# Order of the work at three places of a two-layer decoder trunk: the end of stick-breaking attention, the weight sums of the feed-forward blocks, and the rotary tables

## The chip, the cores and the metric

The kernel runs on one core of one Trainium2 chip. The metric is the device time of one execution in microseconds (us), taken as the median of several runs; lower is better. The core has five engines that this text names by the profile's abbreviations: PE (TensorE, the matrix multiplier), DVE (VectorE), ACT (ScalarE), POOL (GpSimd) and SP (SyncE, which here issues the DMA transfers). Each engine takes its own instructions in the order in which they were put in its list, and waits for others through semaphores.

## The reference

The program is a trunk of two layers on a sequence of 512 tokens of width 1024, all in float32. Each layer is a chain of four sub-layers, each between two RMS norms and added to the residual stream `h`:

- a gated feed-forward block, `silu(x @ w_gate) * (x @ w_up) @ w_down`, with 2816 hidden features, added at half weight
- a token mixer: in the first layer multi-scale retention with rotary queries and keys (4 heads), in the second layer stick-breaking attention (8 heads of 128)
- a second feed-forward block like the first
- a gate on a per-layer input embedding

Stick-breaking attention computes, for a query i and the keys j before it, the scores `z`, the running sums of `log_sigmoid(-z)` from j up to i, and the weights `exp(log_sigmoid(z) + rem)`; the weights times the values give each head's context, and all heads' contexts together are multiplied by one output matrix:

```
log_one_minus = where(mask, log_sigmoid(-z), 0)
rem = cumsum(log_one_minus, reverse) - log_one_minus
a = where(mask, exp(log_sigmoid(z) + rem), 0)
out = concat_heads(a @ v) @ w_out
```

The rotary tables are the sine and the cosine of position times frequency; only retention uses them.

## The kernel before

*Precision.* Each float32 operand is split into a high and a low part (`split`: ACT copies the high part, line 153, and DVE subtracts it from the operand, line 154), and a product is three matmuls, high by high, high by low and low by high (`mm3`, lines 159 to 161). So each weight that comes from memory costs one ACT and one DVE operation on a tile of 128 x 1024 before PE can use it.

*Weights.* `plan` writes down the list of all weight pieces in the order in which PE uses them, and PE's programme takes them from it one by one (`take`). `_fetch` has SP load a piece into one of 8 raw buffers, `_load` splits it into one of 5 buffer pairs (`wh`, `wl`; `HL_BUFS`), and `_ahead` keeps as many pieces loaded as buffers are free: piece n takes the buffers of piece n-5. Some pieces have a home elsewhere in the on-chip memory.

*Feed-forward blocks.* 22 hidden blocks of 128 features are made in pairs 0 to 10. Pair 0 is computed plainly. For pairs 1 to 10 the gate and the up projection use a scheme with seven products instead of eight (`gate_up`, 24 matmuls at line 728 for each product): it needs sums of the input quarters (made once in each block, on DVE, in `pre`) and sums of the pair's four raw weight tiles `b[0, 0]`, `b[1, 0]`, `b[0, 1]`, `b[1, 1]`. The products of a pair come in the order 1, 2, 6, 5, 7, 3, 4. The weight sums are made in `_load` when product 6's piece is loaded: `t1`, and two more in place, three DVE operations on 128 x 1024 (line 247), and a fourth after product 6's split. A product's result is taken from its PSUM bank by an ACT copy or by a DVE add into `y` (line 687), and a bank that holds products 1, 6, 7 and 4 in turn is read after each, so that product 4 can't start before the add of product 7. The down projections of an earlier group of pairs are put between the products of the later pairs (`ffn_steps`).

*Rotary tables.* `rope_tables` makes them with 24 DVE and 3 ACT operations on 128 x 512, from the positions that SP loads, and has SP store them in two DRAM tiles. The call stands at step 50 of the 86 steps of the first layer's first feed-forward block, near the products of pair 6, but nothing that it reads is made there.

*Attention's end.* `last_products` runs when the last head, 7, is left. `sums(7)` makes its running sums, `context(6)` and `context(7)` are the last contexts (`oT`, split by ACT and DVE), and `product(half, t, heads)` multiplies the contexts of the given heads for one row tile t of 128 tokens by their part of the output matrix: three matmuls of 512 columns for each head. Half 0 of the output's columns takes heads 4 to 7, half 1 heads 2 to 7; the heads before were added into `part` earlier. The products of a tile and half go to one PSUM bank. `close_a` ends half 0 of a tile: DVE adds the bank to `part` (line 558), ACT squares and sums (line 524), POOL multiplies by the gain (line 528). `close_b` does the same for half 1 (lines 565, 538, 539) and ends with POOL's power (line 541). `run_c` then does the residual on DVE (line 546) and the next norm's squares on ACT (line 460) and POOL (451, 452), `run_d` the scaling on DVE (line 464), and `flush` the transposes on PE (line 470) that make the input of the next block.

*What sets the order.* A scheduler orders each engine's list when the program is built: an operation is put in the list when its inputs are ready by the scheduler's own times, earlier traced work first. Three things override it: inside `traced` PE keeps the written order; `chained` ties each operation of the norm chains behind the one before it on its engine; and `issue_after(ins)` puts what is traced inside it behind `ins` in the list of the same engine. That is an order of issue and no wait for an end. It doesn't touch other engines.

The loop at the end of attention, as it is before:

```python
for t in range(NT):
    product(0, t, range(4, h))
context(h)
product(1, 0, range(2, h))
for t in range(NT):
    product(0, t, (h,))
    ssa[t] = self.close_a(t, pss[0][t], gpost, False)
self.done_with(2)
for t in range(NT):
    if t:
        product(1, t, range(2, SH - 3))
    self.run_c()
```

Of the kernel before, what the change touches and what calls it, by code (L numbers as in the profile page):

```python
# [21 lines left out]
NT = S // P  # L22
# [25 lines left out]
def ffn_steps():  # L48

    out = [("gu", 1, 1), ("gu", 1, 2), ("down", 0, 0, 0), ("down", 0, 1, 0), ("gu", 2, 1), ("gu", 2, 2)]  # L50
    out += [("gu", p, prod) for p in (1, 2) for prod in ORDER[2:]]
    out += [("gu", 3, prod) for prod in ORDER]
    for g in range(2, len(GROUPS)):
        gu = [("gu", p, prod) for p in range(*GROUPS[g]) for prod in ORDER]
        down = [("down", g - 1, half, q) for half in range(2) for q in range(*GROUPS[g - 1])]
        at = [int((i + 0.7) * len(gu) / len(down)) for i in range(len(down))]
        if g == len(GROUPS) - 1:

            at = [int((i + 0.7) * (len(gu) - 3) / len(down)) for i in range(len(down))]
        for i, x in enumerate(gu):  # L60
            out.append(x)
            out += [d for d, a in zip(down, at) if a == i]
    return out
# [17 lines left out]
class Trunk:  # L81
# [148 lines left out]
    def piece(self, x, w, home=None):  # L230
        if home and home[0] == "blk":
            parts = [self.blk2() for _ in range(2)]
            for i, hl in enumerate(parts):
                self.split(hl, x[:, i * 512 : i * 512 + 512])
            return tuple(Parts(p) for p in zip(*parts))
        if home and home[0] in ("xe", "xs"):
            h, l = (getattr(self, home[0])[:, 2 * home[1] + i] for i in range(2))
        elif home:
            h, l = (self.work.tile([P, 1280], F32R, tag="pk", name="pk", bufs=self.npacks)[:, :w] for _ in range(2))
        else:  # L240
            h = self.hl.tile([P, 1024], F32R, tag="wh", name="wh")[:, :w]
            l = self.hl.tile([P, 1024], F32R, tag="wl", name="wl")[:, :w]
        self.split((h, l), x)
        return h, l

    def sub(self, out, a, b, op=ALU.subtract):
# [2 lines left out]
    def _load(self):  # L249
        n = self.loaded  # L250
        item = self.items[n]
        self._open(n)
        if item[0] == "w":
            x = self.packs.pop(n)
            self.queue[n] = self.piece(x, 1024, self.home.get(n))
        elif item[0] == "st":
            _, key, prod = item
            b = self.packs[key]
            if prod == 6:
                w = b[0, 0].shape[-1]  # L260
                b["t1"] = self.sums.tile([P, 1024], F32, tag="t1", name="t1")[:, :w]

                with self.tc.issue_after(self.s_sums):
                    self.sub(b["t1"], b[0, 1], b[0, 0])
                    self.sub(b[0, 0], b[1, 1], b["t1"])
                    self.sub(b[0, 1], b[1, 1], b[0, 1])
            x = {1: b[0, 0], 2: b[1, 0], 3: b[1, 1], 4: b[0, 0], 5: b.get("t1"), 6: b[0, 0], 7: b[0, 1]}[prod]
            self.queue[n] = self.piece(x, x.shape[-1])
            if prod == 6:
                self.sub(b[0, 0], b[1, 0], b[0, 0])  # L270
        self.loaded += 1
# [413 lines left out]
    def ffn(self, layer, j, gpost, after, side=None):  # L685
# [102 lines left out]
        with self.traced():  # L788
            for n, x in enumerate(ffn_steps()):
                if n == 50 and side:  # L790
                    side()
                (gate_up if x[0] == "gu" else down)(*x[1:])
                if x[:2] == ("gu", NPAIR - 1) and x[2] in ORDER[2:]:
                    self.open_home(self.LAST[ORDER.index(x[2]) - 2])
# [191 lines left out]
    def stick(self, layer, gpost, after):  # L986
# [85 lines left out]
        def sums(h):  # L1072

            b, r = z.pop(h)
            for i, (at, w) in enumerate(BANK):
                group(b[i][:, :w], [(self.ntri, x[:, at : at + w]) for x in L[h]], False)
            for jj in range(1, NT):
                for j in range(jj):
                    group(r[j][:, (jj - j) * P :], [(self.nones, seg(x, jj)) for x in L[h]], False)
            e = pack()  # L1080
            for i, (at, w) in enumerate(BANK):
                nc.scalar.activation(e[:, at : at + w], b[i][:, :w], AF.Exp)
            mask(e)
            a[h] = pack(F32R), pack(F32R)
            self.split(a[h], e)

        def context(h):
            ps = self.ps()
            for j in range(NT):
                vj = [x[:, (j % 2) * 256 + (h % 2) * P : (j % 2) * 256 + (h % 2) * P + P] for x in v[h // 2, j // 2]]  # L1090
                self.mm3(ps[:, j * P :], vj, [seg(x, j) for x in a[h]], j == 0, j == NT - 1)
            oT[h] = self.blk2()
            self.split(oT[h], ps)
# [36 lines left out]
        h = SH - 1  # L1130

        def last_products():
            sums(h)
            pss = [[self.ps() for _ in range(NT)] for _ in range(2)]
            self.open_home(*(("pk", i) for i in range(3)))
            us0 = [self.unit("sb_w_out", idx, 512 + 256 * i, 2, 0, 512) for i in range(2)]
            specs = [("sb_w_out", idx, 256 + 256 * i, 2, 512, 512) for i in range(3)]
            self.begin_chain()
            us1 = [self.unit(*spec) for spec in specs]

            def product(half, t, heads):
                for hd in heads:
                    h0 = 4 - 2 * half
                    u = (us0, us1)[half][(hd - h0) // 2]
                    self.mm3(pss[half][t], stat(hd)(0, t), [x[:, hd % 2, :] for x in u], hd == h0, hd == h)

            for t in range(NT):
                product(0, t, range(4, h))
            context(h)
            product(1, 0, range(2, h))  # L1150
            for t in range(NT):
                product(0, t, (h,))
                ssa[t] = self.close_a(t, pss[0][t], gpost, False)
            self.done_with(2)
            for t in range(NT):
                if t:
                    product(1, t, range(2, SH - 3))
                self.run_c()
                if t == NT - 1:
                    self.flush()  # L1160
                product(1, t, range(SH - 3, SH) if t else (h,))
                if t == NT - 1:
                    self.done_with(3)
                self.close_b(t, pss[1][t], gpost, False, ssa[t], after)
                self.run_d()
                if t == 2:
                    self.flush(1)
            self.run_c()
            self.run_d()

        with self.traced():
            last_products()
# [177 lines left out]
```

## Time and profile before

| | |
|---|---|
| median of 3 runs | 2220.15 us (2218.29 to 2221.09) |
| the profiled execution: its time, its span | 2220.81 us, 2218.9 us |
| PE busy | 2174.7 us, 98% of the span |
| DVE busy | 1466.0 us, 66% |
| ACT busy | 1003.4 us, 45% |
| POOL busy | 236.7 us, 11% |
| mean granted PE clock | 0.995 of full speed |

The span is from the first to the last instruction of one execution. A row of a timeline has the start in us, the duration, the engine, the line, the operation, what it writes and reads by the program's names (`t`, `raw`: weights and their sums; `wh`, `wl`: the split; `xs`, `xe`: the input's quarters and their sums; `y`: results of products), its shape, how many were merged, and in brackets how long the engine stood idle before it and what ended that. Matmuls overlap, so their durations are longer than the distance from one start to the next. A row of the table by stretch gives busy time and number of instructions of PE, PE's weight loads, DVE, ACT and POOL in that stretch, and then the granted PE clock, the share of the DMA engines and their GB/s. A row of a group ends with busy time, mean duration and idle time before. A row of the chain has the start, the length and the work on it.

### The profile page before, as it was taken

Reading aid. Unit: us, or ns where it says so; the run is one execution under the profiler, and the core shown is the slowest. Engines: PE = TensorE matmul, PEld = TensorE weight load, DVE = VectorE, ACT = ScalarE, POOL = GpSimd, SP = SyncE. Lnnn points to the kernel's source line nnn. Section 1 sums busy time; section 2 is a strip of 40 time slices with the busy share of each in tenths; the row PEclk is TensorE's granted clock in tenths of the full one; section 3 lists DMA queues with packets and bytes.
Section 4 is the critical chain, followed back from the end, with each engine's and each line's share of the span. In section 5 each row is a group of like instructions: output and inputs, shape, how many; then the busy total and the mean of one; then the engine's idle time right before and its main releaser. Section 6 shows DMA issues by size and latency. Waiting matters only on the chain.

```text
span 2218.9 us, 32989 instructions
## 1 busy us (share of the span) xinstructions
PE 2174.7 (98%) x13640; PEld 1962.7 (88%) x13640; DVE 1466.0 (66%) x1739; ACT 1003.4 (45%) x1476; POOL 236.7 (11%) x337
## 2 busy tenths in 40 slices
PE   8999999999999999999999999999999989999998
PEld 7899998888888899999988999998988889999986
DVE  7976676553535588577766976776554568767764
ACT  5543444232223355344555544444555455444443
POOL 0000003110111210000032000002131220000031
PEclk9999999999999999999999999999999999999999
DMA  5323335231322324322453233235312232333341
GB/s 214 127 102 97 106 121 181 91 106 60 110 76 81 124 96 134 114 97 94 143 201 131 87 116 112 98 103 171 115 58 77 86 115 95 105 105 105 114 162 57
DMA packets 69415, 248.83 MB, mean 112 GB/s; under 512 B 7952, under 2 KB 7952, under 8 KB 69264
## 3 DMA queue, kind: packets, MB, share of 16 engines
q1 hardware_dynamic: 69264, 246.72, 33.6%
q8 instruction: 107, 1.75, 0.3%
q14 instruction: 44, 0.36, 0.1%
HBM read 229.38 MB, written 17.30 MB: 111 GB/s over the span
## 4 chain that ended last, share of the span: by engine, by line
PE 88%; DVE 6%; ACT 2%; issue 1%; POOL 1%; DMA 1%; SPq 0%; DVEq 0%; POOLq 0%; ACTq 0%
PE ps L728 33%; PE ps L160 18%; PE ps L159 18%; PE ps L161 18%; PE ps L1042 1%; DVE wl L154 1%; DMA raw<-wts 1%; DVE raw L247 1%; DVE xs L154 1%; PE ps L470 1%; DVE part L546 0%; DVE xe L154 0%; DVE y L687 0%; ACT xn L460 0%; POOL st L541 0%
## 5 line engine op out<-in xcount | busy, mean ns | idle before, releaser
L154 DVE TENSOR_TENSOR wl<-raw,wh 128x1024 fp32r<-128x1024 f32 x427 | 526.6, 1239 | 356.2 <-ACT wh L153 353.5
L153 ACT ACTIVATE wh<-raw 128x1024 fp32r<-128x1024 f32 x427 | 449.8, 1059 | 640.5 <-PE ps L728 202.2
L728 PE MATMUL ps<-xs,wh 128*128 128x256 f32 x2560 | 464.7, 283 | 6.7 <-DVE y L687 6.6
L728 PEld LDWEIGHTS ps<-xs,wh 128*128 128x128 f32 x2560 | 399.0, 189 | 11.0 <-DVE y L687 7.9
L728 PE MATMUL ps<-xs,wl 128*128 128x256 f32 x1280 | 362.9, 284 | 0.0
L728 PE MATMUL ps<-xe,wh 128*128 128x256 f32 x1920 | 350.5, 284 | 0.0
L728 PEld LDWEIGHTS ps<-xe,wh 128*128 128x128 f32 x1920 | 302.3, 193 | 1.9
L728 PE MATMUL ps<-xe,wl 128*128 128x256 f32 x960 | 272.8, 284 | 4.3 <-DVE wl L154 4.3
L159 PE MATMUL ps<-wh,blk 128*128 128x512 f32 x680 | 266.3, 392 | 1.9 <-ACT blk L153 1.9
L161 PE MATMUL ps<-wh,blk 128*128 128x512 f32 x680 | 265.2, 391 | 1.1 <-DVE blk L154 1.1
L160 PE MATMUL ps<-wl,blk 128*128 128x512 f32 x680 | 266.0, 391 | 0.0
L728 PEld LDWEIGHTS ps<-xs,wl 128*128 128x128 f32 x1280 | 242.3, 189 | 0.0
L728 PEld LDWEIGHTS ps<-xe,wl 128*128 128x128 f32 x960 | 184.9, 193 | 4.5 <-DVE wl L154 4.5
L160 PE MATMUL ps<-xs,wh 128*128 128x256 f32 (+1 forms) x576 | 186.1, 323 | 2.2 <-DVE xs L154 2.2
L159 PE MATMUL ps<-xs,wh 128*128 128x256 f32 (+1 forms) x576 | 186.5, 324 | 0.2 <-ACT xs L153 0.2
L161 PE MATMUL ps<-xs,wl 128*128 128x256 f32 (+1 forms) x576 | 185.3, 322 | 0.0
L161 PE MATMUL ps<-wh,xs 128*128 128x512 f32 (+1 forms) x448 | 162.9, 364 | 0.0
L159 PE MATMUL ps<-wh,xs 128*128 128x512 f32 (+1 forms) x448 | 162.7, 363 | 0.0
L160 PE MATMUL ps<-wl,xs 128*128 128x512 f32 (+1 forms) x448 | 162.6, 363 | 0.0
L526 POOL TENSOR_SCALAR st<-st 128x1 f32<-128x1 f32 x32 | 8.9, 279 | 1375.0 <-ACT junk L524 1358.9
L161 PEld LDWEIGHTS ps<-wh,blk 128*128 128x128 f32 x680 | 128.0, 188 | 28.7 <-DVE blk L154 1.5
L159 PEld LDWEIGHTS ps<-wh,blk 128*128 128x128 f32 x680 | 128.2, 189 | 26.8 <-ACT blk L153 2.1
(169 smaller groups left out, 3443.8 us busy)
## 6 DMA issues: line engine op xcount, KB each, us to landing
raw<-wts SPq DMA_DIRECT2D x382, 512.0 KB, 3.5
keep<-part SPq DMA_DIRECT2D x28, 512.0 KB, 4.2
rin<-keep SPq DMA_DIRECT2D x28, 512.0 KB, 4.1
gbc<-gains SPq DMA_DIRECT2D x16, 512.0 KB, 3.8
part<-x SPq DMA_DIRECT2D x4, 512.0 KB, 7.7
rin<-x SPq DMA_DIRECT2D x4, 512.0 KB, 4.9
out<-part SPq DMA_DIRECT2D x8, 256.0 KB, 2.2
dec<-decay SPq DMA_DIRECT2D x4, 256.0 KB, 3.7
```

The source lines that it names most:

```text
L153: h = self.nc.scalar.activation(hl[0], x, AF.Copy)
L154: l = self.nc.vector.tensor_tensor(out=hl[1], in0=x, in1=hl[0], op=ALU.subtract)
L159: mm(ps, a[0], b[0], start=start, stop=False)
L160: mm(ps, a[0], b[1], start=False, stop=False)
L161: mm(ps, a[1], b[0], start=False, stop=stop)
L247: self.nc.vector.tensor_tensor(out=out, in0=a, in1=b, op=op)
L470: nc.tensor.transpose(ps[:, c * P : (c + 1) * P], xn[:, (4 * q + c) * P : (4 * q + c + 1) * P], self.ident)
L526: nc.gpsimd.tensor_scalar(out=r, in0=ss, scalar1=1.0, scalar2=(4 if half else 1) * RMS_EPS, op0=ALU.mult, op1=ALU.add)
L728: nc.tensor.matmul(o, w[a][:, g, k, :], x[b][:, k, :], start=new and g + k + n == 0, stop=k == 3 and n == 2, skip_group_check=True)
L1042: nc.tensor.matmul(ps, l, m, start=fresh and i == 0, stop=i == len(pairs) - 1, skip_group_check=True)
```

## The change

Three edits, which add no operation and remove none:

1. The last DVE operation of a split is kept as `last_piece` when a piece goes to ordinary buffers, and a pair's three weight sums are issued behind it on DVE, beside the older tie to the sums of the input (`s_sums`).
2. The rotary tables' operations are issued behind the split that was traced last at their place: its ACT part for the ACT operations, its DVE part for the DVE ones. The DMA issues of SP are not tied.
3. At attention's end PE's order changes: the products of heads 4 and 5 of half 0 come first for all four row tiles, then head 6 of tiles 0 and 1, heads 2 to 5 of half 1 of tile 0, `context(7)`, the rest of head 6, and then the loop over row tiles does half 0's head 7 with `close_a` and half 1 with `close_b` tile by tile, where half 0 was closed for all tiles first.

```diff
@@ piece
         self.split((h, l), x)
+        self.last_piece = self.split_ins[1].ins
         return h, l
@@ _load
-                with self.tc.issue_after(self.s_sums):
+                with self.tc.issue_after(self.s_sums), self.tc.issue_after(self.last_piece):
                     self.sub(b["t1"], b[0, 1], b[0, 0])
                     self.sub(b[0, 0], b[1, 1], b["t1"])
                     self.sub(b[0, 1], b[1, 1], b[0, 1])
@@ ffn
                 if n == 50 and side:
-                    side()
+                    with ExitStack() as stack:
+                        for i in self.split_ins:
+                            stack.enter_context(self.tc.issue_after(i.ins))
+                        side()
@@ last_products
             for t in range(NT):
-                product(0, t, range(4, h))
+                product(0, t, (4, 5))
+            for t in range(2):
+                product(0, t, (6,))
+            product(1, 0, range(2, 6))
             context(h)
-            product(1, 0, range(2, h))
+            for t in range(2, NT):
+                product(0, t, (6,))
+            product(1, 0, (6,))
             for t in range(NT):
                 product(0, t, (h,))
+                if t == NT - 1:
+                    self.done_with(2)
                 ssa[t] = self.close_a(t, pss[0][t], gpost, False)
-            self.done_with(2)
-            for t in range(NT):
                 if t:
                     product(1, t, range(2, SH - 3))
                 self.run_c()
```

## The prediction

> **What bounds the kernel now.** I read the page first, then TensorE's (PE's) timeline for breaks in its stream, then what VectorE (DVE), ScalarE (ACT), GpSimd (POOL) and SyncE (SP) did at each break, and last a table by stretch.
>
> ```profile
> PE 2174.7 (98%) x13640; PEld 1962.7 (88%) x13640; DVE 1466.0 (66%) x1739; ACT 1003.4 (45%) x1476; POOL 236.7 (11%) x337
> ...
> core 0: us, PE busy (x) PEld busy (x) DVE busy (x) ACT busy (x) POOL busy (x), PEclk, DMA share, GB/s
> 64.40:100.90 36.50, 31.82 (x243) 31.21 (x242) 35.03 (x42) 19.44 (x28) 0.00 (x0) 0.91 0.44 145
> 854.90:861.40 6.50, 5.88 (x49) 5.67 (x48) 6.50 (x9) 2.84 (x4) 0.00 (x0) 1.00 0.01 3
> 1250.50:1274.20 23.70, 20.54 (x170) 20.13 (x169) 20.76 (x24) 11.26 (x16) 0.00 (x0) 1.00 0.35 108
> 1870.00:1881.50 11.50, 8.98 (x63) 8.78 (x62) 10.48 (x14) 4.12 (x7) 0.00 (x0) 0.85 0.03 7
> 1757.20:1799.40 42.20, 33.48 (x144) 27.11 (x144) 22.05 (x25) 15.83 (x31) 13.09 (x20) 0.92 0.38 123
> ...
> 858.56 28.83 PE ps L728 x240
> ...
> 1875.67 30.36 PE ps L728 x240
> ```
>
> PE is the bound: it works nearly all the time, so a change pays only where PE stands still. Two rows of the chain give the pace of the feed-forward products, 28.83/240 = 0.120 us a matmul, 2.9 us for the 24 of one product. With it the first four stretches give what PE lost: 36.5 - 243 x 0.120 = 7.3 us; 6.5 - 5.9 = 0.6; 23.7 - 20.4 = 3.3; 11.5 - 7.6 = 3.9. They are the same place in the four feed-forward blocks, where pairs 1 to 3 begin; together 15.1 us. The fifth stretch, attention's end, holds 114 products 512 wide (0.23 us each, rows below), 12 of `context(7)` (about 1.8 us by their widths) and 16 transposes (0.11 us each): 29.6 us of work in 42.2, so 12.6 us lost. All else has no break worth a term. These 27.7 us are the most that this change can win.
>
> **The change part by part.**
>
> *Pair sums behind the last piece.* What PE waits for in the third stretch:
>
> ```profile
> 1253.28 0.28 PE L728 MATMUL ps<-xe,wl 128*128 128x256 f32 x1
> 1255.27 0.39 PE L728 MATMUL ps<-xs,wh 128*128 128x256 f32 x1 [1.71 <-DVE y L687]
> ...
> 1252.26 1.23 DVE L247 TENSOR_TENSOR t<-raw 128x1024 f32<-128x1024 f32 x1 [2.55 <-DMA raw<-wts]
> 1253.40 1.22 DVE L154 TENSOR_TENSOR wl<-t,wh 128x1024 fp32r<-128x1024 f32 x1
> 1254.53 0.68 DVE L687 TENSOR_TENSOR y<-y,ps 128x512 f32<-128x512 f32 x1
> ...
> 1264.82 1.23 DVE L247 TENSOR_TENSOR t<-raw 128x1024 f32<-128x1024 f32 x1 [1.19 <-DMA raw<-wts]
> ...
> 1869.18 1.23 DVE L247 TENSOR_TENSOR t<-raw 128x1024 f32<-128x1024 f32 x1 [2.27 <-DMA raw<-wts]
> ```
>
> DVE runs in order. At 1249.7 it stood before `t1` of pair 3, whose weights had not landed; behind it waited a split of pair 2 and the add `y` that empties the bank in which PE must go on (product 4 of pair 1 after product 7). `t1` of pair 3 is needed eight products later, 8 x 2.9 = 23 us. Twice more the same: 1264.82 (pair 4) and 1869.18. With the tie, pair 3's three sums follow the split of (3, 2). That split takes the buffer that PE frees when it ends (2, 5), so it can't be early: without the break PE starts (1, 4) at 1253.4 and ends (2, 5) three products on, at 1262.1, and the split follows at about 1263.5; pair 3's weights have landed by 1252.3. So the DMA waits leave DVE's path, and the break with them. The new price: three sums of 1.14 us pitch and the split of product 6 now come in a row. From (2, 5)'s end: ACT's `wh` 1.06, split 1.14, `t1` to +3.6; `y` of (2, 7) is ready at about +3.1 and due at +5.7, so it goes in after `t1`, before the two sums that need `t1` finished. The sixth product's split ends at about +8, due at +14. No break follows by these numbers; if `y` went behind all three sums it would be 0.9 late. I take 0.2 in each block. From pair 4 on, down-projections of 5.5 us lie between, or the buffer comes free one product later, after `y`. Taken: 0.6 + 3.3 + 3.9 - 0.6 = 7.2 us (bounds 3.3, the three DMA waits of the rows less 0.9 in each block, to 7.8).
>
> *Rotary tables.*
>
> ```profile
> 64.41 0.40 PE L728 MATMUL ps<-xe,wh 128*128 128x256 f32 x2
> 69.09 0.58 PE L728 MATMUL ps<-xe,wl 128*128 128x256 f32 x1 [4.28 <-DVE wl L154]
> 69.47 0.63 PE L728 MATMUL ps<-xe,wh 128*128 128x256 f32 x2
> ...
> 57.65 2.37 DVE L247 TENSOR_TENSOR t<-raw 128x1024 f32<-128x1024 f32 x2
> 63.99 1.24 DVE L247 TENSOR_TENSOR raw<-raw,t 128x1024 f32<-128x1024 f32 x1
> 67.80 1.24 DVE L154 TENSOR_TENSOR wl<-raw,wh 128x1024 fp32r<-128x1024 f32 x1
> ...
> L410 DVE SCALAR_TENSOR_TENSOR rope<-rope x10: 686/694/706, 30.1 to 74.9; 128x512 f32<-128x512 f32 x10
> L406 DVE TENSOR_SCALAR rope<-rope x4: 417/425/437, 28.7 to 66.3; 128x512 f32<-128x512 f32 x4
> ...
> 29.00:69.00 40.00, 35.28 (x251) 32.99 (x250) 39.93 (x60) 25.77 (x38) 0.00 (x0) 0.98 0.09 30
> 220.00:240.00 20.00, 20.00 (x138) 18.65 (x138) 13.73 (x17) 8.12 (x12) 0.00 (x0) 1.00 0.42 132
> 240.00:260.00 20.00, 20.00 (x147) 19.04 (x146) 16.85 (x20) 8.70 (x12) 0.00 (x0) 1.00 0.17 56
> ```
>
> DVE has almost no idle time from 29 to 69 us, and PE waits 4.28 us at 69.09 for the split of (1, 6) at 67.80. Ahead of that split, in the saturated time, stand some 17 table operations (eight or so of L410 at 0.6 us pitch, the rest at 0.34: about 8 us) and pair 2's three sums (3.4 us, one of the two at 57.65, and those at 63.99 and behind it). Both go away: the split would come some 11 us sooner, bounded by what feeds it, and is due at 64.5. PE's wait goes, and so does the slow stretch behind it (granted clock 0.91 over the window). DVE then has slack up to pair 3: 7.3 us won, less 0.2 as above (bounds 4.3, the wait alone, to 7.3).
> The tables' 24 DVE and 3 ACT operations, 10.7 us of DVE pitch, and SP's two stores go behind the split of hidden block 13, at about 221 us now. There DVE idles 6.3 and 3.1 us in 20, and PE's pieces are five ahead; the first reader is retention, 120 us on. The loading of the positions isn't tied. A residual load that needs the tables' buffer waits longer, but is read only after 330 us. Cost 0.3 (0 to 2; without cover it would be 10.7).
>
> *Attention's end.*
>
> ```profile
> 1757.10 0.27 PE L161 MATMUL ps<-pk,blk 128*128 128x128 f32 x1
> 1759.29 0.50 PE L159 MATMUL ps<-wh,blk 128*128 128x512 f32 x1 [1.92 <-ACT blk L153]
> 1761.13 0.79 PE L161 MATMUL ps<-wh,blk 128*128 128x512 f32 x1 [1.10 <-DVE blk L154]
> ...
> 1785.39 0.39 PE L160 MATMUL ps<-pk,blk 128*128 128x512 f32 x1
> 1785.62 0.39 PE L161 MATMUL ps<-pk,blk 128*128 128x512 f32 x1
> 1789.50 1.06 PE L470 MATMUL ps<-ident,xn 128*128 128x128 f32 x8 [3.50 <-DVE xn L464]
> 1794.86 1.97 PE L470 MATMUL ps<-ident,xn 128*128 128x128 f32 x8 [2.21 <-DVE xn L464]
> ...
> L528 POOL TENSOR_TENSOR part<-part,gbc 128x512 f32<-128x512 f32 x4 | 5.2, 1298 | 0.3
> ...
> 1784.36 1.28 DVE L546 SCALAR_TENSOR_TENSOR part<-part,st,rin 128x1024 f32<-128x1024 f32 x1 [3.89 <-POOL st L541]
> 1789.80 1.29 DVE L546 SCALAR_TENSOR_TENSOR part<-part,st,rin 128x1024 f32<-128x1024 f32 x1 [0.44 <-POOL st L541]
> ```
>
> First wait: head 6's context is split at 1759 to 1761.1, and PE asks for it at 1757.3 after six products of heads 4 and 5. Moving the other 18 products of heads 4 and 5 (18 x 0.23 = 4.1 us) ahead brings that to 1761.4: both waits go, and the half-speed products behind them. Head 7's split then has 2.1 us of cover (three times three products of head 6). PE reaches head 7's first product at about 1769.3 instead of 1774.2: 4.9 us.
> Second wait: the norm of row tile 0. Its chain (L558, the squares, L528, L541, L546, the next norm's square, L464, transposes) now waits behind four L528 on POOL; interleaved, behind one. I laid the new order out with the durations of these rows, each engine in order. L546 of tile 0 falls at 1774.6 to 1775.5 (first or later duration of L541, 0.55 or 1.48), 9 to 10 us sooner; the turns to tiles 1 and 2 are 5.7 and 6.9 us, since L558, a square and L528 join each (now 5.4 and 6.1). PE has only 5.7 us a turn, so it still waits about 0.4 us at tile 0's transposes, 2 at tile 1's and 2 at the start of the next block. That block starts about 8.3 us sooner than now.
> ```profile
> 1872.88 0.28 PE L728 MATMUL ps<-xe,wl 128*128 128x256 f32 x1
> 1875.67 0.50 PE L728 MATMUL ps<-xs,wh 128*128 128x256 f32 x2 [2.52 <-DVE y L687]
> 1877.63 0.63 PE L728 MATMUL ps<-xs,wh 128*128 128x256 f32 x2
> ```
> A break of 2.8 us brought half speed here and 1.5 us more on 240 products (30.36 against 28.83); the breaks of 2.0 and 1.7 in the third stretch brought none (clock 1.00). The two new ones of 2 us lie between: I take 0.3. The Trainium skill (TensorE: Matmul & The Clock Gate, HAM oscillation) has the abstract rule of no idle gaps over about 3.4 us. By it the new breaks would cost no clock, and the sum would be 0.3 better; the trace disagrees at 2.8 us. So 8.0 us (bounds 3.0, the first two waits alone, to 12.6; no loss, since the products are the same and every chain starts sooner).
>
> *Sum.* 7.2 + 7.1 - 0.3 + 8.0 = 22.0 us. Against the profiled execution's own 2220.81 that is 2198.8; the median of the runs is 0.66 lower, so 2198.1, rounded to 2198.5.
>
> **The rivals.**
> *A, half of it comes.* The static order shifts with every edit, and a new small wait takes the place of some breaks: `y` 0.9 late in each block, an oT split or the norm chain 4 us later than laid out. For it: DVE is busy 20.8 of 23.7 us in the third stretch, little room. Against: the tie touches only work due 15 us later. 22 - 4 x 0.7 - 4 - 3 (at the first block) = 12.2 us: 2208.
> *B, slower: sums in a row hold back `y`.* If the sums go ahead of the add that empties bank a in every pair, not once in a block, PE waits 0.9 us or more in each of nine pairs, of four blocks: 36 x 0.9 = 32 against 22, so 2230. It decides from 0.6 us a pair. For it: sums that today fill idle time anywhere now lie in one place. Against: by the buffers' turn only pair 3's can collide.
> *C, the tie does nothing.* If weights, not order, were late in stretches 2 to 4, those 7.2 us stay: 2205.5. Against: the waits on `t1` are for a pair that PE doesn't need yet.
>
> **How the numbers follow.** Forecast 0.58, A 0.22, C 0.08, B 0.07, and 0.05 for no change (gains lost to new waits). The range reaches from 2192 (all bounds at their best give 27.7 off, 2192.5) to 2213 (all at their worst: 3.3 + 4.3 - 2 + 3.0 = 8.6 off, 2211.5), which takes in A and C; the forecast's own is 2192 to 2205. A measurement of this kernel tells 0.2% (4.4 us) from no change. Faster 0.88, within 0.05, slower 0.07.
>
> **What would show it.** Right: no DVE wait for `raw<-wts` at `t` in the first 60 us of a block; PE unbroken at (1, 6) of the first block; the rope rows after 210 us; PE unbroken between `context(6)` and the first transposes; the first L546 of attention's end about 5 us after head 7's first product. Wrong: `y L687` as a releaser of PE in pairs beyond the third, breaks between 210 and 270 us, or a wait of PE on `blk L153` before head 6 or 7.

## The result, and the profile after

| | before | after |
|---|---|---|
| median of 4 runs each | 2219.4 us (2218.29 to 2221.09) | 2194.36 us (2193.93 to 2194.80) |
| ratio, 95% interval | | 0.9887 (0.9869 to 0.9904) |
| profiled execution: time, span | 2220.81, 2218.9 us | 2193.93, 2192.1 us |

The change makes the kernel 25.0 us faster by the medians; between the two profiled executions the span falls by 26.8 us. Forecast were 2198.5 us, in a range of 2192 to 2213. The lines that this text names stand one further down in the changed kernel: the weight sums are L248, the add into `y` L688, the seven-product matmuls L729, the table operations L400 to L445, the transposes L471; those that close the norms move by one as well.

First the line of busy times on the page and the table by stretch, of the kernel after. The five stretches start and end at the same matmuls as those of before (the counts, which take in matmuls that reach over an end of the stretch, differ by one at most).

```profile
PE 2164.9 (99%) x13640; PEld 1955.5 (89%) x13640; DVE 1460.0 (67%) x1739; ACT 1002.6 (46%) x1476; POOL 236.9 (11%) x337
```
```profile
core 0: us, PE busy (x) PEld busy (x) DVE busy (x) ACT busy (x) POOL busy (x), PEclk, DMA share, GB/s
63.00:91.78 28.78, 28.78 (x243) 28.78 (x242) 25.79 (x30) 15.64 (x23) 0.00 (x0) 1.00 0.44 145
845.61:851.22 5.61, 5.61 (x49) 5.61 (x48) 5.61 (x7) 2.85 (x4) 0.00 (x0) 1.00 0.01 3
1240.32:1260.39 20.07, 20.07 (x171) 20.07 (x169) 18.06 (x23) 11.04 (x16) 0.00 (x0) 1.00 0.31 106
1847.66:1854.81 7.15, 7.15 (x62) 7.15 (x61) 7.15 (x10) 4.18 (x7) 0.00 (x0) 1.00 0.00 0
1743.79:1776.52 32.73, 29.84 (x144) 24.21 (x142) 21.75 (x25) 14.89 (x31) 12.81 (x19) 1.00 0.46 152
```

In the first four stretches PE is busy for the whole length, at full clock: nothing is left to win there. In the fifth it still stands for 2.9 us.

To see where the 26.8 us come from I laid the two traces on each other matmul by matmul and read by how much the same matmul starts earlier. The kernel after has gained 0.7 us by 25 us, 1.4 by 50 us, 9.2 at the end of the first block, 10.2 behind pairs 1 to 3 of the second block, 13.9 behind those of the third, 22.4 at the end of attention and 26.8 behind pairs 1 to 3 of the last. So the parts are 9.2 (first block), 0.9 + 3.7 + 4.3 = 8.9 (the later three) and 8.5 (attention's end). "Gain in a stretch" below always means this comparison.

The weight sums of pair 3 in the third block, DVE's timeline after:

```profile
1253.00 1.23 DVE L154 TENSOR_TENSOR wl<-raw,wh 128x1024 fp32r<-128x1024 f32 x1 [0.42 <-ACT wh L153]
1254.14 1.22 DVE L248 TENSOR_TENSOR t<-raw 128x1024 f32<-128x1024 f32 x1
1255.28 0.68 DVE L688 TENSOR_TENSOR y<-y,ps 128x512 f32<-128x512 f32 x1
1255.88 1.22 DVE L248 TENSOR_TENSOR raw<-raw,t 128x1024 f32<-128x1024 f32 x1
1257.01 1.22 DVE L248 TENSOR_TENSOR raw<-raw 128x1024 f32<-128x1024 f32 x1
```

`t1` comes right behind the split, waits for no DMA, and the add `y` goes in between `t1` and the two sums, in the order that the prediction gave. The waits of DVE for weights in the kernel before (us in total, times, longest us):

```profile
DVE t L247 <- DMA raw<-wts: 11.1, 12, 2.6
DVE raw L247 <- DMA raw<-wts: 4.8, 11, 0.8
```

In the kernel after DVE has no such wait left.

The rotary tables after (groups of their operations, median duration, first and last start) lie between 215 and 266 us; and the end of attention shows on DVE and on PE:

```profile
L411 DVE SCALAR_TENSOR_TENSOR rope<-rope x10: 678/683/693, 225.2 to 260.7; 128x512 f32<-128x512 f32 x10
L445 ACT ACTIVATE rope<-rope x1: 615/615/615, 265.1 to 265.1; 128x512 f32<-128x512 f32 x1
```
```profile
1756.94 0.69 DVE L559 TENSOR_TENSOR part<-part,ps 128x512 f32<-128x512 f32 x1 [1.46 <-PE ps L161]
...
1761.29 1.28 DVE L547 SCALAR_TENSOR_TENSOR part<-part,st,rin 128x1024 f32<-128x1024 f32 x1
...
1766.81 1.28 DVE L547 SCALAR_TENSOR_TENSOR part<-part,st,rin 128x1024 f32<-128x1024 f32 x1
...
1773.52 1.28 DVE L547 SCALAR_TENSOR_TENSOR part<-part,st,rin 128x1024 f32<-128x1024 f32 x1
```
```profile
1748.34 0.50 PE L161 MATMUL ps<-wh,blk 128*128 128x512 f32 x1 [0.28 <-DVE blk L154]
...
1771.86 1.09 PE L471 MATMUL ps<-ident,xn 128*128 128x128 f32 x8 [1.15 <-DVE xn L465]
...
1776.52 0.38 PE L159 MATMUL ps<-xs,wh 128*128 128x256 f32 x1 [1.47 <-ACT xs L153]
1777.24 0.39 PE L160 MATMUL ps<-xs,wh 128*128 128x256 f32 x1 [0.34 <-DVE xs L154]
```

From the first add of a closing (1756.94) to the first residual operation (1761.29) pass 4.4 us; before they were 9.2 (1775.2 to 1784.36). The four rows of PE are all its waits from the last contexts to the next block: 0.28, 1.15, 1.47 and 0.34 us.

### The profile page after: what moved, and what is told of

Same layout as the page of the kernel before. It is cut to its first block, busy times and chain, and to the rows that moved or that the text cites. A ratio compares the mean times of both kernels' runs of the same rounds, so it can differ in the third digit from the quotient of the medians.

```text
span 2192.1 us, 32947 instructions
## 1 busy us (share of the span) xinstructions
PE 2164.9 (99%) x13640; PEld 1955.5 (89%) x13640; DVE 1460.0 (67%) x1739; ACT 1002.6 (46%) x1476; POOL 236.9 (11%) x337
## 4 chain that ended last, share of the span: by engine, by line
PE 92%; DVE 3%; ACT 2%; issue 1%; POOL 1%; DMA 0%; SPq 0%; POOLq 0%; DVEq 0%; ACTq 0%
PE ps L729 36%; PE ps L160 18%; PE ps L159 18%; PE ps L161 18%; PE ps L1046 1%; PE ps L471 1%; DVE xs L154 1%; DVE part L547 0%; ACT xn L461 0%; PE ps L939 0%; POOL st L542 0%; POOL pk L1039 0%; DMA part<-x 0%; ACT junk L539 0%; ACT xs L153 0%
## 5 line engine op out<-in xcount | busy, mean ns | idle before, releaser
L729 PE MATMUL ps<-xs,wh 128*128 128x256 f32 x2560 | 462.4, 282 | 0.0
L729 PEld LDWEIGHTS ps<-xs,wh 128*128 128x128 f32 x2560 | 397.8, 189 | 3.1
L729 PE MATMUL ps<-xs,wl 128*128 128x256 f32 x1280 | 362.2, 283 | 0.0
L729 PE MATMUL ps<-xe,wh 128*128 128x256 f32 x1920 | 348.7, 283 | 0.0
L729 PEld LDWEIGHTS ps<-xe,wh 128*128 128x128 f32 x1920 | 300.8, 192 | 1.9
L729 PE MATMUL ps<-xe,wl 128*128 128x256 f32 x960 | 271.6, 283 | 0.0
L729 PEld LDWEIGHTS ps<-xs,wl 128*128 128x128 f32 x1280 | 241.3, 189 | 0.0
L729 PEld LDWEIGHTS ps<-xe,wl 128*128 128x128 f32 x960 | 183.8, 192 | 0.0
```

Source lines behind the costliest of these rows:

```text
L729: nc.tensor.matmul(o, w[a][:, g, k, :], x[b][:, k, :], start=new and g + k + n == 0, stop=k == 3 and n == 2, skip_group_check=True)
```

## The experiments

The theory: DVE's order is the cause in the feed-forward blocks (an operation that is not needed yet waits for a DMA, and the add that empties PE's bank stands behind it; in the first block 8 us of table operations and 3.4 us of sums stand in front of a split). At attention's end two things add up: PE's arrival at head 7, and four gain multiplies ahead of the first power on POOL. The main rivals are late weights instead of order (C in the prediction), and a norm chain that sets the end whatever PE does.

**Edit 1 alone** (`sums_only`)

```diff
@@ piece
+        self.last_piece = self.split_ins[1].ins
@@ _load
-                with self.tc.issue_after(self.s_sums):
+                with self.tc.issue_after(self.s_sums), self.tc.issue_after(self.last_piece):
```


> Edit 1 alone on the kernel before (a pair's weight sums behind its last piece). In the changed kernel's trace the later blocks gave 0.9, 3.7 and 4.3 us against before where pairs 1 to 3 begin. Theory: these 8.9 us come back whole, and in the first block pair 2's three sums (3.4 us of DVE) leave the front of the split that PE waited 4.28 us for, so that wait falls to about 0.9 us and the slow clock behind it goes: 5 to 6 us there. Sum about 14.5: 2204 to 2205 us. Rival (the weights are late, not the order): nothing in blocks 2 to 4, about 2214.

Measured 2206.62 us (ratio 0.994, 0.9926 to 0.9953), 13.6 us below the 2220.18 beside it, where 14.5 were expected. The three later blocks gain 0.9, 3.7 and 4.3 us, as in the whole change; so order was the cause there, and rival C falls. The first block gains 6.2 by its end. There PE's wait doesn't shrink to 0.9 us but to 1.68, since table operations still stand between the sums and the split (PE's row and two of DVE's):

```profile
66.08 0.39 PE L729 MATMUL ps<-xe,wl 128*128 128x256 f32 x1 [1.68 <-DVE wl L154]
```
```profile
62.46 0.41 DVE L407 TENSOR_SCALAR rope<-rope 128x512 f32<-128x512 f32 x1
...
64.81 1.22 DVE L154 TENSOR_TENSOR wl<-raw,wh 128x1024 fp32r<-128x1024 f32 x1
```

**Edit 1 for pairs 3 and 4 only** (`sums_34`)

```diff
@@ piece
+        self.last_piece = self.split_ins[1].ins
@@ _load
-                with self.tc.issue_after(self.s_sums):
+                with self.tc.issue_after(self.s_sums), (
+                        self.tc.issue_after(self.last_piece) if key[2] in (3, 4) else nullcontext()):
```


> Edit 1 for pairs 3 and 4 only; the other pairs keep the order before. Theory: the add that empties PE's bank was behind sums of pairs 3 and 4 that waited for weights, so blocks 2 to 4 gain the same 8.9 us as with the whole edit; in the first block pair 2's sums stay in front of the late split, so it gains little (0 to 2 us). About 2209 to 2211. Rival (other pairs' sums matter as well): less than 6 us in blocks 2 to 4, 2214 or more.

Measured 2209.22 us (0.9954, 0.9941 to 0.9966). The later blocks again gain 0.9, 3.7 and 4.3 us: all of it lies in pairs 3 and 4. The other pairs still wait for weights, 20 times and for 9.6 us in all, and it costs nothing:

```profile
DVE raw L248 <- DMA raw<-wts: 6.7, 14, 1.1
DVE t L248 <- DMA raw<-wts: 2.9, 6, 0.9
```

In the first block PE's wait at 67.82 us is 4.26 us, as before, since pair 2's sums and the tables are still in front of it. Its stretch gains 1.8 us even so; 0.8 of them come from the clock, which was halved for 3.41 us behind this wait and for 6.83 us in the trace of before.

**Edit 2 alone** (`rope_only`)

```diff
-                    side()
+                    with ExitStack() as stack:
+                        for i in self.split_ins:
+                            stack.enter_context(self.tc.issue_after(i.ins))
+                        side()
```


> Edit 2 alone (rotary tables tied to a split at 220 us). Theory: the table operations alone are some 8 us of DVE in front of the split that PE waited 4.28 us for, so without them the wait is gone even with pair 2's sums in place; the first block ends about 8.5 to 9 us sooner, all else as before: about 2211. Then the gains of edits 1 and 2 in the first block overlap, and the parts add up to more than the whole. Rival (pair 2's sums are what holds that split): at most 4 us, 2215 or more.

Measured 2213.63 us (0.9971, 0.9961 to 0.9982): 6.6 us, between theory and rival. The mechanism is the theory's: the wait for the split of product 6 is gone with pair 2's sums in place, 6.2 us of gain in the stretch where the whole change gains 7.8; the block ends 8.0 us sooner in this trace, where 8.5 to 9 were expected. But in the same block, with the sums still untied, DVE waits for weights at two sums, and PE for the add behind them:

```profile
89.93 0.51 PE L728 MATMUL ps<-xs,wh 128*128 128x256 f32 x2 [1.12 <-DVE y L687]
```
```profile
71.21 1.23 DVE L247 TENSOR_TENSOR t<-raw 128x1024 f32<-128x1024 f32 x1 [0.76 <-DMA raw<-wts]
...
83.44 1.22 DVE L247 TENSOR_TENSOR t<-raw 128x1024 f32<-128x1024 f32 x1 [0.86 <-DMA raw<-wts]
```

**Edit 3 alone** (`end_only`: the changed `last_products` in the kernel before)

> Edit 3 alone (order of attention's end). Theory: independent of the other two, the same 8.5 us as in the changed kernel's trace, with all else as before: about 2211. Rival (part of those 8.5 us came from the other edits by way of the static order): 4 to 6 us, 2214 to 2216.

Measured 2210.69 us (0.9959, 0.9947 to 0.9972), 9.5 us; in the stretch itself the gain is 8.5 us, the same as in the whole change. The parts' medians fall by 13.6, 6.6 and 9.5 us, 29.6 together, and the whole by 24.5 to 26 (the median of before lies between 2218.7 and 2220.4 beside the different runs). The overlap is in the first block: its stretch from 63 us gains 5.8 with edit 1, 6.2 with edit 2 and 7.8 with both, 4.3 less than the sum.

**The changed kernel with the tie of pairs 3 and 4 only** (`after_34`, the edit of `sums_34` put into the kernel after), beside **the changed kernel once more** (`after_again`)

> The changed kernel with the weight sums tied in pairs 3 and 4 only (in pair 2 and in pairs 5 to 10 as before the change). Theory: edits 1 and 2 overlap in the first block, where the tables' move alone removes PE's wait for the split of product 6, and the rest of edit 1 lies in pairs 3 and 4: 0 to 0.5 us against the changed kernel, 2194 to 2195. Rival (the tie in other pairs has a share of its own): 1.5 us or more slower.

> The changed kernel itself once more, as the base on this chip for the three runs beside it: 2194 to 2195.

Measured 2194.55 us (2193.81 to 2194.93) and 2194.19 us (2193.94 to 2194.40). No difference: with the tables out of the way, no gain of the tie of pair 2 and of pairs 5 to 10 can be measured.

**Edit 3 in two halves** (`end_products`: its order of products with the old closes; `end_interleave`: the closes tile by tile with the old order of products)

```diff
@@ end_products
-                product(0, t, range(4, h))
+                product(0, t, (4, 5))
+            for t in range(2):
+                product(0, t, (6,))
+            product(1, 0, range(2, 6))
             context(h)
-            product(1, 0, range(2, h))
+            for t in range(2, NT):
+                product(0, t, (6,))
+            product(1, 0, (6,))
@@ end_interleave
                 product(0, t, (h,))
+                if t == NT - 1:
+                    self.done_with(2)
                 ssa[t] = self.close_a(t, pss[0][t], gpost, False)
-            self.done_with(2)
-            for t in range(NT):
```


> Edit 3's order of products alone on the kernel before: heads 4 and 5, head 6 of two tiles and half 1's heads 2 to 5 ahead of the last context; the closes stay as before (half 0 of all four tiles first). Theory: PE reaches head 7's first product 4.9 us sooner, and the chain of norms, which starts there, shifts with it: 4.9 us, about 2215. Rival (the chain of norms is held by POOL's four gain operations and not by PE's arrival): 0 to 2 us, 2218 to 2220.

> Edit 3's closing alone: each row tile's half 0 and half 1 closed in turn, with the products of heads 4 to 7 in the order before. Theory: the rest of the 8.5 us, 3.5 to 4: the first residual operation comes some 4 us sooner after head 7's first product, with the two waits at the last context unchanged: about 2216. Rival (the gains don't add, the chain is bound at one place): 0 to 1.5 us or over 6 us.

Measured 2215.47 us (0.998, 0.9971 to 0.9989) and 2216.74 us (0.9984, 0.9975 to 0.9993). In the stretch of attention's end the first gains 4.3 us and the second 2.8, read at the start of the next block; right behind it half a clock took some 1 to 1.5 us of the 2.8 back (last section). The groups of the first add and of the residual on DVE, `end_products` first, then `end_interleave` (first and last start):

```profile
L558 DVE TENSOR_TENSOR part<-part,ps x4: 686/687/689, 1771.0 to 1773.1; 128x512 f32<-128x512 f32 x4
...
L546 DVE SCALAR_TENSOR_TENSOR part<-part,st,rin x4: 1278/1284/1285, 1780.2 to 1799.9; 128x1024 f32<-128x1024 f32 x4
```
```profile
L558 DVE TENSOR_TENSOR part<-part,ps x4: 675/679/687, 1776.2 to 1792.2; 128x512 f32<-128x512 f32 x4
...
L546 DVE SCALAR_TENSOR_TENSOR part<-part,st,rin x4: 1280/1282/1284, 1780.5 to 1800.8; 128x1024 f32<-128x1024 f32 x4
```

With the products' order alone everything comes 4.3 us sooner and the 9.2 us from the add to the residual stay; with the closes alone these shrink to 4.3. Both theories hold, and both rivals fall. The halves make 7.1 of 8.5 us. The other 1.4 are the clock's: in `end_interleave` the first add comes 1.4 us later than in before, counted from where the stretch begins, though the two waits at the last context are the same 1.9 and 1.1 us. Behind them the granted clock was 0.50 for 6.83 us, and for 3.41 us in before. The table by stretch (columns as above), of before, `end_interleave` and `no_gain`, the next run:

```profile
1760.00:1768.00 8.00, 6.90 (x25) 5.58 (x25) 3.34 (x4) 1.13 (x2) 0.00 (x0) 0.79 0.58 199
1760.00:1768.00 8.00, 7.23 (x20) 5.71 (x21) 2.99 (x4) 0.78 (x1) 0.00 (x0) 0.59 0.59 199
1760.00:1768.00 8.00, 6.29 (x26) 4.91 (x27) 4.66 (x5) 2.45 (x4) 0.00 (x0) 1.00 0.56 183
```

**Without POOL's gain multiplies** (`no_gain`: the kernel before without the four multiplies by the norm's gain on half 0)

```diff
-        nc.gpsimd.tensor_tensor(out=a, in0=a, in1=g[:, :512], op=ALU.mult)
+        if not getattr(self, 'no_gain', False):
+            nc.gpsimd.tensor_tensor(out=a, in0=a, in1=g[:, :512], op=ALU.mult)
@@ last_products is traced with self.no_gain = True
```


> The kernel before, in which POOL's multiply by the norm's gain is left out for half 0 of the output at stick-breaking attention's end (four operations of 1.30 us; the output lacks that gain there). Theory: these four stand in POOL's list ahead of the first power and hold the first residual operation; without them it comes 3 to 4 us sooner, PE's waits at the transposes shrink by as much: about 2216. Rival (the squares on ACT, or DVE, hold it): 0 to 1 us, 2219.

Measured 2216.08 us (0.9982, 0.9973 to 0.9991); in the stretch the gain is 4.6 us. Not all of it is the multiplies': 1.4 us are there at the first add already, since behind the same two waits the clock wasn't halved at all in this trace (third row above). The multiplies' share is from the first add to the first residual, where 5.9 us are left of 9.2; these 3.3 us are within the 3 to 4 that were expected:

```profile
L559 DVE TENSOR_TENSOR part<-part,ps x4: 687/688/689, 1775.1 to 1777.2; 128x512 f32<-128x512 f32 x4
...
L547 DVE SCALAR_TENSOR_TENSOR part<-part,st,rin x4: 1277/1284/1286, 1781.0 to 1800.7; 128x1024 f32<-128x1024 f32 x4
```

So these multiplies, on an engine that is busy 11% of the time, did hold the path to the next block's first product, for 3.3 us.

**The tables made twice** (`rope_twice`, on the kernel after)

```diff
                             stack.enter_context(self.tc.issue_after(i.ins))
                         side()
+                        side()
```


> The changed kernel with the rotary tables' operations made twice in a row at their new place (another 24 DVE and 3 ACT operations, 10.7 us of DVE pitch). Theory (they are covered there: DVE idles 6.3 and 3.1 us in the 20 us slices from 220, and PE's pieces are split several ahead): 0 to 0.6 us against the changed kernel, 2194 to 2195. Rival (no cover): a few us up to 10.7, to 2205, with waits of PE for a split between 220 and 260 us.

Measured 2196.17 us (2195.68 to 2196.29), 1.8 us above the kernel after; more than the theory's 0.6 and far from 10.7. (The kernel after wasn't run beside it.) PE isn't disturbed between 220 and 326 us. The second set is spread over what idle time DVE has, down to the block's last products, and there it is in the way of the last hidden block's tail:

```profile
L440 DVE TENSOR_SCALAR rope<-rope x2: 422/426/429, 261.0 to 326.2; 128x512 f32<-128x512 f32 x2
...
L445 ACT ACTIVATE rope<-rope x2: 614/622/631, 264.6 to 328.3; 128x512 f32<-128x512 f32 x2
```
```profile
332.71 0.50 PE L159 MATMUL ps<-xs,blk 128*128 128x512 f32 x1 [1.15 <-ACT blk L153]
```

That wait is 0.39 us in the kernel after: some 0.8 us between these two traces come from the tables. Another 1.0 us comes from a half clock behind attention's end, where the breaks are those of the kernel after (last section); whether the other runs of `rope_twice` had it too no trace shows.

**A further step** (`context_sooner`, `context_flush`, on the kernel after)

```diff
@@ context_sooner
                 product(0, t, (4, 5))
-            for t in range(2):
-                product(0, t, (6,))
-            product(1, 0, range(2, 6))
             context(h)
-            for t in range(2, NT):
-                product(0, t, (6,))
-            product(1, 0, (6,))
+            product(0, 0, (6,))
+            product(1, 0, range(2, SH - 1))
             for t in range(NT):
+                if t:
+                    product(0, t, (6,))
                 product(0, t, (h,))
@@ context_flush, besides
-                self.run_c()
                 if t == NT - 1:
                     self.flush()
+                self.run_c()
```


> The changed kernel with the last context right after the products of heads 4 and 5, then head 6 of tile 0 and half 1 of tile 0, and head 6 of the other tiles inside the loop, each just ahead of its head 7. Theory: PE reaches head 7's first product about 2 us sooner (nine matmuls of 0.23 us less ahead of it) and the chain of norms moves with it, since tiles 1 to 3 have waiting time for their three more matmuls: 2 us, about 2192.4. Rival (the later tiles are bound by PE after all, or head 6's context is late again for the last context's place): 0 to 0.5 us, or a new wait of PE at that context and slower by 1 us.

> As the run with the earlier context, and for the last tile the transposes of the tiles before are put ahead of the residual of tile 2 in the written order, so that the split of the next block's first input comes in ACT's list ahead of that tile's squares. Theory: PE's wait at the start of the next block (1.63 and 0.60 us in the changed kernel) shrinks by up to 2 us on top: 2190 to 2191. Rival (the norm of tile 3, not tile 1's input, sets the start): the same as the run with the earlier context, or slower by what tile 2's norm loses.

Measured 2191.77 us (2191.41 to 2192.18) and 2191.66 us (2191.10 to 2192.30), beside 2194.19 us for the kernel after. The first is the theory's 2 us and a little more: it is 2.4 us faster than the kernel after, and the waits at the last context and at tile 1's transposes are gone; what is left is the start of the next block:

```profile
1774.59 0.38 PE L159 MATMUL ps<-xs,wh 128*128 128x256 f32 x1 [1.02 <-ACT xs L153]
1775.31 0.39 PE L160 MATMUL ps<-xs,wh 128*128 128x256 f32 x1 [0.34 <-DVE xs L154]
```

The second does what it says there (ACT's splits of the input come sooner, PE's wait at the block's first products is gone), but the wait turns up again 14 us later, where PE asks for the next tiles:

```profile
1788.19 0.38 PE L159 MATMUL ps<-xs,wh 128*128 128x256 f32 x1 [0.94 <-ACT xs L153]
1788.91 0.39 PE L160 MATMUL ps<-xs,wh 128*128 128x256 f32 x1 [0.34 <-DVE xs L154]
```

The rival holds: not tile 1's input but the norm of the later tiles is last, and both kernels end alike.

## Why the prediction was right, point by point

*What bounds the kernel.* Right. All the gain is breaks of PE that went, and the first four stretches have none left. The 27.7 us that it called the most to be won were not quite that: 1.4 of the 26.8 us lie outside the five stretches.

*Pair sums, 7.2 us.* Right in mechanism and place (`sums_only`, `sums_34`); it measured 8.9 between these two traces. The term was 1.7 us too small for two reasons. The price of 0.2 us a block for a late `y` never came: `y` goes in behind `t1`, as the row at 1255.28 shows. And the work in the three windows was counted too high, by some 1.1 us: the table's 49, 170 and 63 matmuls take in those that reach over an end of the window. Only 47, 168 and 60 start in it, and 0.119 us each is what the kernel after needs there. The size is no constant either. The same stretches of the second, third and fourth block (us between the same matmuls) in the traces of kernels that keep the old order of sums, and of two that don't:

```
                2nd     3rd     4th     sum
before          6.50   23.74   11.45   41.7
rope_only       7.46   22.94    9.84   40.2
end_only        7.46   22.40    8.45   38.3
end_products    7.24   22.60    9.67   39.5
end_interleave  6.98   22.29    8.75   38.0
no_gain         7.42   23.98    8.98   40.4
sums_only       5.61   20.07    7.16   32.8
after           5.61   20.07    7.15   32.8
```

With the old order the breaks cost 5.2 to 8.9 us, by the execution (that this goes by how late the weights land would fit, and isn't shown); the profile of before, from which the term was read, is at the top. Without them the three stretches are the same to 0.01 us. The forecast of 7.2 was nearer to the middle of these than the difference of the two profiles is.

*Rotary tables, 7.1 us and a cost of 0.3.* Right in mechanism, and too small: the stretch gained 7.8, since its 243 matmuls were counted like those above, where 241 start in it, and the 0.2 for a late `y` never came; and the first block gained 9.2 in all. Of the rest, 0.7 us is a wait that the prediction didn't see. In the trace of before, two table operations stood in front of a split of the input on DVE at 30.05, and PE waited (DVE's rows, then PE's):

```profile
30.05 1.42 DVE L410 SCALAR_TENSOR_TENSOR rope<-rope 128x512 f32<-128x512 f32 x2
31.39 0.68 DVE L154 TENSOR_TENSOR xs<-ps,xs 128x512 fp32r<-128x512 f32 x1
```
```profile
32.13 0.39 PE L160 MATMUL ps<-xs,wh 128*128 128x256 f32 x1 [0.54 <-DVE xs L154]
```

`rope_only` gains the same 0.7 us there, and `sums_only`, `sums_34` and `end_only` nothing. The last 0.7 us, in the first 25, belong to no edit: the same point lies 1.1 and 1.2 us sooner in `end_only` and `sums_34`, which change nothing ahead of it, and 0.2 later in `end_products`. It goes with the clock's first rise. In before, PE's first products start every 0.21 us up to 19.8 us and every 0.12 us from there on; in the kernel after the change comes at 18.2 us, in `end_only` and `sums_34` at 17.2, in `end_products` at 20.3. So these 0.7 us are the luck of two executions. The cost at the new place was nothing, as taken within its bounds; the cover was named too tightly, since the operations fill single gaps from 215 to 266 us. `rope_twice` shows how far it reaches: to about the block's end.

The prediction costed what edits 1 and 2 do in the first block as one term, and so counted the wait of 4.28 us once. That was right, but it didn't say how the term divides: the tables' move alone removes that wait, the sums' tie alone only 2.6 us of it.

*Attention's end, 8.0 us.* Right: 8.5. By steps: the arrival at head 7 was to come 4.9 us sooner and came 4.3 sooner (the first add, 1756.94 against 1775.17 less the 13.9 gained ahead of it); the first L546 9 to 10 us sooner, measured 9.1; the turns 5.7 and 6.9 us, measured 5.5 and 6.7; at tile 0's transposes 0.4 were to be left, measured none; at tile 1's 2, measured 1.15 of waiting (1.3 lost against the pace); at the next block 2, measured 1.47 and 0.34 (2.2 lost). The 0.3 us for a clock that falls behind the new breaks was 0 in this trace, and 1.0 in another of the same breaks. The half clock behind the two old waits, which went with them, isn't the same in every execution either (1.4 us more or less in the two traces above).

*The rivals.* A (half of it eaten by new small waits) didn't come about for the whole change; in `rope_only` one such wait came, the 1.12 us at 89.93. B (`y` held back in every pair) has no trace: PE never waits for `y` after. C (late weights) falls with `sums_only`. Of the signs named for being right, one isn't met to the letter: between `context(6)` and the first transposes PE still waits once, 0.28 us at 1748.34 for the low part of head 6's split, and not for ACT.

The span fell by 26.8 us where the sum said 22.0; the sum's own time is 2198.1, and the 2198.5 on record stands 0.4 above it. The 4.8 us are: 1.7 at the sums, 0.7 in the first block's stretch, 0.7 at 31 us, 0.7 at the start (the clock), 0.5 at attention's end, 0.3 for the cost that didn't come, and 0.2 in small differences and rounding. No term had the wrong sign, and no mechanism was another; the late `y` alone, a small price, didn't come.

## What to carry to other kernels

An engine that takes its list in order pays for an operation that is put in the list too early as much as for one that comes too late: when a wait on a busy engine ends with a DMA, look who stands behind the waiting operation, and when its result is really due. Where two edits clear the same wait, their gains measured alone add up to more than both together. In a chain that crosses engines, four small operations on an engine that is otherwise idle can set the end (3.3 us here); closing one tile completely before the next starts takes them off the path.

## What the runs showed of the hardware that was not expected

The half clock doesn't follow from the length of a break. In the kernel after and in `rope_twice`, attention's end has the same breaks (1.15 and 1.17 us at the transposes, then 1.47 and 0.34 in both) and PE is busy for the same 4.5 of 7.47 us; behind them the granted clock was 1.00 in one and 0.50 for 3.3 us in the other. The table by stretch (columns as above), of `rope_twice` and then of the kernel after:

```profile
1771.03:1778.50 7.47, 4.49 (x24) 3.17 (x23) 5.77 (x9) 3.40 (x8) 4.18 (x7) 1.00 0.60 202
1778.60:1781.90 3.30, 3.30 (x17) 3.30 (x17) 2.39 (x3) 0.72 (x2) 1.82 (x2) 0.50 0.33 115
```
```profile
1770.33:1777.80 7.47, 4.51 (x24) 3.19 (x23) 5.77 (x9) 3.37 (x8) 4.16 (x7) 1.00 0.58 206
1777.90:1781.20 3.30, 3.30 (x30) 3.30 (x29) 2.36 (x3) 0.72 (x2) 1.85 (x2) 1.00 0.27 103
```

In 3.30 us 17 matmuls ran at half clock and 30 at full clock. `end_interleave` has the half clock too, `end_only` hasn't, with the same breaks. `after_34` and `after_again` haven't either. So such a pattern costs 0 or some 1 to 1.5 us by the execution; with two of these six traces halved, that is 0.3 to 0.5 in the mean, and the 0.3 of the prediction stands at its low end.

The clock changes on a grid. In each of the fourteen traces the recorded changes of the granted clock lie whole multiples of 3.41 us apart, counted from its first rise, and between that rise and the end of PE's work each half-clock stretch lasts 3.41 or 6.83 us. The rise itself comes anywhere from 17.2 to 20.3 us. Behind the same waits the clock was halved for 0, 3.41 or 6.83 us at the last context (`no_gain`, before, `end_interleave`), and for 3.41 or 6.83 us in the first block (`sums_34`, before). The Trainium skill (TensorE: Matmul & The Clock Gate, Part 1) describes a free-running window of 3413 ns over which PE's activity is judged; the traces agree with that, in that the changes lie on a grid of 3.41 us and the same breaks went both ways. The rule in the same page's section on HAM oscillation, no idle gaps over about 3.4 us, is once more not enough in these traces: here no gap was over 1.5 us of idle time.

With the old order of sums the runs of the kernel before spread from 2217.9 to 2225.5 us, and those of the changed kernel from 2193.9 to 2194.8. The breaks whose length hangs on a DMA's landing differ by 3.7 us between the six traces above; that they are the cause of the spread fits, but no run isolates it. The clock is the rival: between its first rise and the end of PE's work it was halved for 17.1 us in before and `end_interleave`, 10.2 in `rope_only` and `end_products`, 6.8 in `no_gain` and 3.4 in `end_only`, and not at all in the traces of `after` and `after_again`.
